# The MLP products of a two-layer decoder trunk by Strassen's scheme, up and down as two phases

## The chip, the cores and the metric

The kernel runs on one core of a Trainium2 chip. The metric is the time of one execution on the device in microseconds (us). The engines are named as the profile names them: PE multiplies matrices (PEld is its weight load), DVE, ACT and POOL work element by element, SP only issues DMAs here.

## What is computed

Two layers over 1024 positions of width 1024; the change touches the MLP at the end of each.

```python
for l in range(DEPTH):                      # DEPTH = 2, D_MODEL = 1024, D_FF = 4096
    h = rms_norm(x, norm1[l])
    proj = h @ w_in[l]                      # pool | gate u, v | q, k, v
    ...                                     # pooling, spatial gate, stick-breaking attention
    x = x + jnp.concatenate([ya, yb, yc], axis=-1) @ w_out[l]
    h = rms_norm(x, norm2[l])
    x = x + jnp.square(jax.nn.relu(h @ w_up[l])) @ w_down[l]
return rms_norm(x, final_norm)
```

All data are float32. Each product is computed from operands split in two float32r parts, a high and a low one, as three products: high by high, high by low, low by high.

## The kernel before

Everything is held transposed: a tile has 128 channels on the partitions and 512 positions (half `c`, 1 or 0) in its free dimension, so x is 8 x 2 tiles (`k`, `c`). `mm3` issues the three matmuls of 128 x 128 weights by a 128 x 512 tile into one PSUM bank for each contraction tile. Weights come as 512 KB tiles `raw` through SP (two buffers); `split` makes the high part on ACT (`copy`) and the low part on DVE (`tensor_sub`). The order on each engine is set by the Tile scheduler from the program order and priorities (`early`); it is fixed when the kernel is built, and each engine runs its list in order.

`out_proj(0, second)` is the last step before the MLP: for each of 16 (m, c), twelve matmuls into a bank `po`, then DVE adds the residual (L731), ACT and DVE make the scaled high and low parts that the MLP will read (`put_x`, L115 and L117), ACT squares and POOL adds the square to the running sum `rbc` (L136), from which `rms` later makes the norm of every position.

The MLP runs 8 groups of 4 hidden tiles of 128. For each hidden tile `f` and half `c` there are 24 matmuls into a bank `pj` (`proj`), DVE evacuates with relu and the norm (L776), ACT squares (L780), POOL squares as well (L781), DVE subtracts (L783). Then, for each output tile (m, c), twelve matmuls over the group's four hidden tiles into a bank `po`, and DVE adds the bank to the residual tile `xa` (L800). In one layer that is 1536 matmuls up and 1536 down. The banks rotate: `pj` 2, `po` 4, `pg` 2. In the very last group the positions are split in three pieces (`TAIL`), so that the final norm of one overlaps the products of the next.

## Time and profile before

| | |
|---|---|
| median of 3 runs | 2351.18 us (2351.13 to 2353.78) |
| profiled execution, its own time | 2353.58 us |
| its span in the trace | 2351.9 us |
| TensorE's mean granted clock | 0.984 |
| PE busy | 2268.2 us, 96% of the span |
| DVE, ACT, POOL busy | 54%, 31%, 35% |
| moved by DMA | 118.41 MB |

A profile's groups give, for a line, an engine and an operation, the number of instructions, the mean time of one, and what ended the idle time ahead of them. A busy PE counts a matmul from its start to the end of its pipeline, so the time between two starts, not the duration, is what one more matmul costs. The windows give the busy time of each engine in a stretch.

### The profile page before, as it was taken

How to read it: one execution, taken by the hardware profiler on the slowest of the kernel's cores; microseconds unless marked ns; L12 is line 12 of the kernel's file. 1: busy time of each engine (PE TensorE's matmuls, PEld its weight loads, DVE VectorE, ACT ScalarE, POOL GpSimd, SP SyncE). 2: the span in 40 equal slices, each digit the busy share in tenths (PEclk: the TensorE clock that was granted, in tenths of full speed). 3: DMA queues.
4: the chain of work that ended last, by engine and by line, in shares of the span. 5: the costliest groups of instructions: out<-in, count | busy, mean ns of one | idle time of the engine just before them, and what ended most of it. 6: DMA issues, size and time to landing. Idle time of an engine off the chain costs nothing.

```text
span 2351.9 us, 28573 instructions
## 1 busy us (share of the span) xinstructions
PE 2268.2 (96%) x11224; PEld 1917.9 (82%) x11224; DVE 1264.1 (54%) x1606; ACT 725.5 (31%) x1321; POOL 824.4 (35%) x889
## 2 busy tenths in 40 slices
PE   7999989999999999999999898999999999999997
PEld 5988887788888888888888887878888888888887
DVE  8787769842342342342558777796433433332334
ACT  5556553430120120121446555434110110120121
POOL 7667656430110110111347767464110110110115
PEclk9999999999999999999999998999999999999998
DMA  3000103120220120120301010131210210220211
GB/s 126 28 28 28 42 19 95 54 81 9 63 72 15 58 72 18 54 72 19 125 19 45 11 45 24 41 90 45 72 47 28 69 55 27 63 63 19 63 36 72
DMA packets 40247, 118.41 MB, mean 50 GB/s; under 512 B 5040, under 2 KB 7600, under 8 KB 40112
## 3 DMA queue, kind: packets, MB, share of 16 engines
q1 hardware_dynamic: 38448, 114.48, 15.9%
q8 instruction: 88, 1.44, 0.3%
q10 hardware_dynamic: 1664, 2.10, 0.2%
q14 instruction: 47, 0.39, 0.1%
HBM read 108.17 MB, written 8.39 MB: 50 GB/s over the span
## 4 chain that ended last, share of the span: by engine, by line
PE 79%; DVE 9%; POOL 6%; issue 3%; ACT 2%; DMA 0%; SPq 0%; POOLq 0%; DVEq 0%; ACTq 0%
PE pj L191 13%; PE pj L196 13%; PE pj L197 13%; PE po L197 12%; PE po L196 12%; PE po L191 11%; DVE s L372 3%; POOL a L375 2%; PE t L393 2%; PE av L403 1%; PE av L404 1%; POOL s L365 1%; POOL a L365 1%; PE z L356 1%; PE z L357 1%
## 5 line engine op out<-in xcount | busy, mean ns | idle before, releaser
L781 POOL TENSOR_TENSOR tmp<-tmp 128x512 f32<-128x512 f32 x128 | 177.4, 1386 | 1125.3 <-ACT ah L780 1118.1
L196 PE MATMUL pj<-xl,wh 128*128 128x512 f32 x1344 | 525.4, 391 | 2.8 <-DVE xl L117 2.8
L191 PE MATMUL pj<-xh,wh 128*128 128x512 f32 x1344 | 526.1, 391 | 0.0
L197 PE MATMUL pj<-xh,wl 128*128 128x512 f32 x1344 | 524.9, 391 | 0.0
L191 PE MATMUL po<-ah,dh 128*128 128x512 f32 (+1 forms) x1056 | 402.0, 383 | 1.2 <-DVE xa L800 1.2
L197 PE MATMUL po<-ah,dl 128*128 128x512 f32 (+1 forms) x1056 | 401.9, 383 | 0.0
L196 PE MATMUL po<-al,dh 128*128 128x512 f32 (+1 forms) x1056 | 401.9, 383 | 0.0
L800 DVE TENSOR_TENSOR xa<-po,xa 128x512 f32<-128x512 f32 (+1 forms) x264 | 177.8, 675 | 412.2 <-PE po L197 412.0
L780 ACT ACTIVATE ah<-tmp 128x512 fp32r<-128x512 f32 x128 | 80.3, 628 | 728.3 <-DVE tmp L776 728.3
L196 PEld LDWEIGHTS pj<-xl,wh 128*128 128x128 f32 x1344 | 253.0, 188 | 54.9 <-DVE xl L117 3.7
L197 PEld LDWEIGHTS pj<-xh,wl 128*128 128x128 f32 x1344 | 252.7, 188 | 51.4
L191 PEld LDWEIGHTS pj<-xh,wh 128*128 128x128 f32 x1344 | 253.0, 188 | 51.0
L375 POOL TENSOR_TENSOR a<-a,s 128x255 f32<-128x255 f32 (+1 forms) x192 | 221.3, 1155 | 28.7 <-DVE s L372 21.2
L191 PEld LDWEIGHTS po<-ah,dh 128*128 128x128 f32 x1056 | 198.5, 188 | 40.1 <-DVE xa L800 1.4
L196 PEld LDWEIGHTS po<-al,dh 128*128 128x128 f32 x1056 | 198.6, 188 | 38.6
L197 PEld LDWEIGHTS po<-ah,dl 128*128 128x128 f32 x1056 | 198.6, 188 | 38.6
L776 DVE SCALAR_TENSOR_TENSOR tmp<-pj,rbc 128x512 f32<-128x512 f32 x124 | 85.5, 689 | 207.7 <-PE pj L197 197.9
L108 ACT CAST wh<-raw 128x1024 fp32r<-128x1024 f32 x116 | 121.8, 1050 | 204.4 <-PE pj L196 146.9
L109 DVE TENSOR_TENSOR wl<-raw,wh 128x1024 fp32r<-128x1024 f32 x116 | 154.2, 1329 | 33.1 <-ACT wh L108 32.3
L783 DVE TENSOR_TENSOR al<-tmp,ah 128x512 fp32r<-128x512 f32 x128 | 90.1, 705 | 146.0 <-POOL tmp L781 146.0
L372 DVE TENSOR_TENSOR_SCAN s<-s 128x256 f32<-128x256 f32 (+3 forms) x128 | 132.3, 1041 | 54.4 <-POOL s L365 52.9
L108 ACT CAST dh<-raw 128x1024 fp32r<-128x1024 f32 x64 | 67.2, 1049 | 206.7 <-DMA raw<-in_w_down 206.7
(169 smaller groups left out, 3547.5 us busy)
## 6 DMA issues: line engine op xcount, KB each, us to landing
raw<-in_w_up SPq DMA_DIRECT2D x64, 512.0 KB, 3.6
raw<-in_w_down SPq DMA_DIRECT2D x64, 512.0 KB, 3.6
raw<-in_w_in SPq DMA_DIRECT2D x36, 512.0 KB, 3.6
raw<-in_w_out SPq DMA_DIRECT2D x16, 512.0 KB, 3.6
tmp<-in_xT SPq DMA_DIRECT2D x16, 256.0 KB, 2.7
xd<-xa SPq DMA_DIRECT2D x16, 256.0 KB, 2.0
tmp<-xd SPq DMA_DIRECT2D x16, 256.0 KB, 2.7
a<-in_xT SPq DMA_DIRECT2D x12, 256.0 KB, 5.3
```

What stands on the lines that cost most here:

```text
L108: nc.scalar.copy(hi, src)
L109: nc.vector.tensor_sub(lo, src, hi.bitcast(F32))
L191: mm = nc.tensor.matmul(ps, ah, bh, start=first and i == 0, stop=False)
L196: nc.tensor.matmul(ps, ah, bl, start=False, stop=False)
L197: nc.tensor.matmul(ps, al, bh, start=False, stop=last and i == n - 1)
L372: nc.vector.tensor_tensor_scan(sl, sl, sl, 1.0 if prev is None else prev[:, CH - 1 : CH], ALU.mult, ALU.bypass)
L375: nc.gpsimd.tensor_mul(a[:, lo + 1 : CH], a[:, lo + 1 : CH], s[:, lo : CH - 1])
L776: nc.vector.scalar_tensor_tensor(out=r, in0=ps, scalar=0.0, in1=rbc[c], op0=ALU.max, op1=ALU.mult)
L780: nc.scalar.activation(h, r, AF.Square)
L781: nc.gpsimd.tensor_mul(r, r, r)
L783: nc.vector.tensor_sub(lo, r, h.bitcast(F32))
L800: nc.vector.tensor_add(x, ps, x)
```

## The change

**Products.** A 2 x 2 block product of weights A (A11, A12, A21, A22) and data B takes seven block products, where it took eight: the seven of the Winograd form of Strassen's scheme. They are listed in `STEPS`, each with its accumulating bank (X, Y, Z), the weight block and the data block:

```diff
+STEPS = (
+    ("X", 0, "A11", "B11"), ("Y", 0, "A12", "B21"), ("X", 1, "S2", "T2"), ("Z", 0, "S1", "T1"),
+    ("X", 2, "S3", "T3"), ("Z", 1, "S4", "B22"), ("X", 3, "A22", "T4"),
+)
```

X takes four of them in a row and is read out after each, before the next is added to it (`skip_group_check`). S1 to S4 are sums of weight blocks, made on POOL (`load_a`); T1 to T4 are sums of data blocks.

**Up phase.** An *up step* takes two hidden tiles (A: 2 hidden by 2 channel tiles; B: 2 channel tiles by 2 halves): 7 x 12 = 84 matmuls where two hidden tiles took 96. There are 16 in a layer. The four output blocks of hidden activations, and T1 to T4 for the next phase, are written to DRAM (`hid`), seven tiles of 256 KB a step.

**Down phase.** A *down step* takes four hidden tiles by half of the output tiles, again 84 matmuls for 96; there are 16 in a layer, two to a group. It reads seven tiles of 256 KB back and splits them (`load_b`). Products are added to accumulators in SBUF (`add_to`); the results in Y and Z go through an ACT copy and are added on POOL (`lent`). In the second layer the last group is left as it was (`classic`), because of its `TAIL`.

**Ahead of the MLP.** `second` writes the residual to DRAM and makes seven blocks for each pair of channel tiles (B11, B21, B22 and T1 to T4) where `put_x` made four. The low parts of T1 to T4 are made on POOL (L839).

```diff
+            def load_a(srcs, n):
+                for src in srcs:
+                    raws.append(per.tile([P, D], F32, tag="raw", name=nm("raw"), bufs=2))
+                    nc.sync.dma_start(raws[-1].rearrange("p (f c) -> p f c", f=src.shape[1]), src)
...
+                with early(W_EARLY):
+                    split(*room("w", ("A11", "A12"), per, 2, turns), top)
+                    s12 = ex.tile([P, D], F32, tag="s", name=nm("s12"), bufs=1)
...
+                    nc.gpsimd.tensor_add(s1, a2[:, 0], a2[:, 1])
+                    nc.gpsimd.tensor_sub(s2, s1, a1[:, 0])
+                    split(*room("w", ("S1", "S2"), per, 2), s12)
+                    s3 = tmp()
+                    nc.gpsimd.tensor_sub(s3.rearrange("p (n w) -> p n w", n=n), a1[:, 0], a2[:, 0])
+                    split(*room("u", ("S3",), mw, 1), s3)
+                    nc.gpsimd.tensor_sub(a2[:, 0], s2, a1[:, 1])
+                    split(*room("v", ("S4", "A22"), mw, 1, turns), low)
...
+            def second(m, c, ps):
+                x = t512("xa", 6, F32, xs_)
+                nc.vector.tensor_add(x, ps, x1[m, c])
+                nc.sync.dma_start(xmid[m, c], x)
+                add_sq(m, c, x)
...
+                    t = t512("xt", 3, F32, xs_)
+                    nc.vector.scalar_tensor_tensor(out=t, in0=src, scalar=g, in1=in1, op0=ALU.mult, op1=op)
+                    nc.scalar.copy(h, t)
+                    nc.gpsimd.tensor_sub(lo, t, h.bitcast(F32))
...
+                    def hidden(b, src, c):
+                        r, h = ct(), ct()
+                        nc.vector.scalar_tensor_tensor(
+                            out=r, in0=src, scalar=0.0, in1=rbc[c], op0=ALU.max, op1=ALU.mult
+                        )
+                        nc.gpsimd.tensor_mul(h, r, r)
...
+                            if (bank, i) == ("X", 0):
+                                kept["P1"] = keep(ps)
+                            elif bank == "Y":
+                                t = ct()
+                                nc.vector.tensor_add(t, ps, kept["P1"])
+                                hidden("B11", t, 1)
+                            elif (bank, i) == ("X", 1):
+                                kept["U2"] = keep(ps)
...
+                                    mixed("T1", "B11", "B12", nc.vector.tensor_sub)
+                                    mixed("T2", "B22", "T1", nc.vector.tensor_add)
+                                    mixed("T3", "B22", "B12", nc.vector.tensor_sub)
...
+                def load_b(fp, names):
+                    for b in names:
+                        raw = t512("hr", 4, F32, md)
+                        nc.sync.dma_start(raw, hid[fp, b])
+                        h, lo = out[b] = block_tiles(b)
+                        with early(EVAC_EARLY):
+                            split(h, lo, raw)
+                def add_to(m, c, ps, sign, lent):
+                    x = acc_[m, c]
+                    eng, src = nc.vector, ps
+                    if lent:
+                        eng, src = nc.gpsimd, tmp()
+                        nc.scalar.copy(src, ps)
+                    (eng.tensor_add if sign > 0 else eng.tensor_sub)(x, x, src)
```

**Where it moves instructions.** In all, PE has 8688 of the matmuls that `mm3` issues where it had 9432. Three places show the new order. On PE, in the up phase of the first layer, before: the end of one hidden tile's 24 matmuls (bank `pj_6448`) and the start of the next (`pj_6480`, another bank):

```order
L191 MATMUL pj_6448<-xh_5111,wh_6373 128x512
L196 MATMUL pj_6448<-xl_5113,wh_6373 128x512
L197 MATMUL pj_6448<-xh_5111,wl_6374 128x512
L191 MATMUL pj_6480<-xh_4808,wh_6373 128x512 [waits DVE_49]
L196 MATMUL pj_6480<-xl_4810,wh_6373 128x512
L197 MATMUL pj_6480<-xh_4808,wl_6374 128x512
```

After, at a like place in the up phase: the end of X's second product (S2 in `wh_6134`, T2 in `eh`) and the start of its third (S3 in `uh_6140`, T3):

```order
L210 MATMUL po_6231<-eh_5369,wh_6134 128x512
L215 MATMUL po_6231<-el_5370,wh_6134 128x512
L216 MATMUL po_6231<-eh_5369,wl_6135 128x512
L210 MATMUL po_6231<-eh_5021,uh_6140 128x512 [waits Activation_49]
L215 MATMUL po_6231<-el_5022,uh_6140 128x512
L216 MATMUL po_6231<-eh_5021,ul_6141 128x512
```

The two products now stand back to back on the same bank, with a wait for ACT's copy of the first between them; 30 of the 32 up steps have this pair so.

On DVE, in the down phase of the first layer, before (`xa` is the residual tile, `al`, `wl` and `dl` are low parts):

```order
L109 TENSOR_TENSOR dl_7588<-raw_7586,dh_7587 128x1024
L783 TENSOR_TENSOR al_7534<-tmp_7529,ah_7531 128x512
L776 SCALAR_TENSOR_TENSOR tmp_7561<-pj_7536,rbc_5174 128x512
L109 TENSOR_TENSOR wl_7818<-raw_7816,wh_7817 128x1024
L783 TENSOR_TENSOR al_7566<-tmp_7561,ah_7563 128x512
L800 TENSOR_TENSOR xa_4785<-po_7592,xa_4785 128x512
L800 TENSOR_TENSOR xa_4827<-po_7620,xa_4827 128x512
```

After (L127 are low parts of weights, `wl`, `ul`, `vl`, and of tiles read back, `hr`; L993 are additions to an accumulator):

```order
L993 TENSOR_TENSOR acc_8061<-acc_8061,po_9355 128x512
L127 TENSOR_TENSOR wl_9419<-s_2044_9415,wh_9418 128x1024
L993 TENSOR_TENSOR acc_8065<-acc_8065,po_9358 128x512
L127 TENSOR_TENSOR el_9688<-hr_9685,eh_9687 128x512
L127 TENSOR_TENSOR ul_9425<-tmp_9422,uh_9424 128x512
L127 TENSOR_TENSOR el_9848<-hr_9845,eh_9847 128x512
L127 TENSOR_TENSOR xl_9854<-hr_9851,xh_9853 128x512
L993 TENSOR_TENSOR acc_8035<-acc_8035,po_9539 128x512
L993 TENSOR_TENSOR acc_8059<-acc_8059,po_9355 128x512
L993 TENSOR_TENSOR acc_8039<-acc_8039,po_9542 128x512
L127 TENSOR_TENSOR xl_9866<-hr_9863,xh_9865 128x512
```

The additions that free the banks stand between splits, where they had stood alone in long rows; a down step has 8 of them, 8 splits of 512 and 3 of 1024.

On POOL, in `out_proj(0, second)`, before (the two running sums in turn):

```order
L136 TENSOR_TENSOR rbc_4791<-rbc_4791,tmp_4833 128x512
L136 TENSOR_TENSOR rbc_4812<-rbc_4812,tmp_4855 128x512
L136 TENSOR_TENSOR rbc_4791<-rbc_4791,tmp_4883 128x512
L136 TENSOR_TENSOR rbc_4812<-rbc_4812,tmp_4905 128x512
L136 TENSOR_TENSOR rbc_4791<-rbc_4791,tmp_4927 128x512
```

After (L154 is the running sum, L839 a low part of T1 to T4, L794 a sum of weight blocks):

```order
L839 TENSOR_TENSOR xl_5084<-xt_5085,xh_5083 128x512
L154 TENSOR_TENSOR rbc_4959<-rbc_4959,tmp_5128 128x512
L839 TENSOR_TENSOR el_5136<-xt_5137,eh_5135 128x512
L839 TENSOR_TENSOR el_5142<-xt_5143,eh_5141 128x512
L794 TENSOR_TENSOR s_1115_5400<-raw_5394 128x512
L154 TENSOR_TENSOR rbc_4937<-rbc_4937,tmp_5175 128x512
L839 TENSOR_TENSOR el_5148<-xt_5149,eh_5147 128x512
```

POOL's list there grows from 14 additions to 34 instructions (14 sums, 16 low parts, 4 sums of weight blocks), and the sums that the norm needs stand behind low parts.

## Rows read from the trace of the kernel before

**Rows 1.** Page: span; busy us (share of the span), instructions of an engine.

```profile
span 2351.9 us, 28573 instructions
...
PE 2268.2 (96%) x11224; PEld 1917.9 (82%) x11224; DVE 1264.1 (54%) x1606; ACT 725.5 (31%) x1321; POOL 824.4 (35%) x889
```

**Rows 2.** Windows: stretch in us, busy us and instructions of each engine, clock, DMA.

```profile
core 0: us, PE busy (x) PEld busy (x) DVE busy (x) ACT busy (x) POOL busy (x), PEclk, DMA share, GB/s
438.00:480.00 42.00, 42.00 (x186) 34.20 (x185) 32.79 (x38) 23.31 (x36) 20.11 (x15) 1.00 0.18 51
800.00:1000.00 200.00, 200.00 (x884) 165.65 (x883) 70.05 (x90) 25.51 (x32) 22.34 (x16) 1.00 0.14 43
1190.00:1215.00 25.00, 22.46 (x140) 19.71 (x141) 16.02 (x25) 14.25 (x30) 12.96 (x22) 0.93 0.15 43
...
500.00:1190.00 690.00, 690.00 (x3049) 571.64 (x3047) 258.08 (x328) 117.58 (x155) 105.65 (x79) 1.00 0.18 55
```

**Rows 3.** Timeline, DVE, down products: start us, duration us, instruction, [idle before <-releaser].

```profile
536.73 0.69 DVE L800 TENSOR_TENSOR xa<-po,xa 128x512 f32<-128x512 f32 x1 [2.03 <-PE po L197]
539.45 0.69 DVE L800 TENSOR_TENSOR xa<-po,xa 128x512 f32<-128x512 f32 x1 [2.03 <-PE po L197]
```

**Rows 4.** Groups by line and shape: xcount | busy us, mean ns | idle before.

```profile
L191 PE MATMUL po<-ah,dh 128*128 128x512 f32 x992 | 383.7, 389 | 0.0
...
L800 DVE TENSOR_TENSOR xa<-po,xa 128x512 f32<-128x512 f32 x248 | 171.3, 691 | 402.7 <-PE po L197 402.6
...
L783 DVE TENSOR_TENSOR al<-tmp,ah 128x512 fp32r<-128x512 f32 x128 | 90.1, 705 | 146.0 <-POOL tmp L781 146.0
...
L109 DVE TENSOR_TENSOR dl<-raw,dh 128x1024 fp32r<-128x1024 f32 x64 | 78.4, 1226 | 62.1 <-ACT dh L108 62.1
```

**Rows 5.** Timeline, second layer's `rms`: a PSUM bank handed from PE to ACT.

```profile
1641.05 1.05 PE L163 MATMUL pg<-ident,rst 128*128 128x128 f32 x8
...
1642.19 0.59 ACT L165 COPY rbc<-pg 128x512 f32<-128x512 f32 x1 [9.52 <-PE pg L163]
```

**Rows 6.** Timeline, second layer's attention: a PSUM bank handed back from ACT to PE.

```profile
1206.71 0.38 ACT L362 ACTIVATE a<-z 128x256 f32<-128x256 f32 x1
...
1207.14 0.33 PE L356 MATMUL z<-kx,qh 128*128 128x128 f32 x1 [0.40 <-ACT a L362]
```

**Rows 7.** Timeline, DVE in `out_proj(0, second)` of the first layer.

```profile
443.23 0.74 DVE L117 SCALAR_TENSOR_TENSOR xl<-xa,cs,xh 128x512 fp32r<-128x512 f32 x1
443.89 0.68 DVE L731 TENSOR_TENSOR xa<-po,xh 128x512 f32<-128x512 f32 x1
444.49 4.58 DVE L117 SCALAR_TENSOR_TENSOR xl<-xa,cs,xh 128x512 fp32r<-128x512 f32 x3
...
451.13 0.69 DVE L731 TENSOR_TENSOR xa<-po,xh 128x512 f32<-128x512 f32 x1
```

**Rows 8.** Timeline, POOL in the same stretch.

```profile
443.47 5.05 POOL L136 TENSOR_TENSOR rbc<-rbc,tmp 128x512 f32<-128x512 f32 x3 [6.74 <-ACT tmp L132]
451.10 1.30 POOL L136 TENSOR_TENSOR rbc<-rbc,tmp 128x512 f32<-128x512 f32 x1 [2.57 <-ACT tmp L132]
```

**Rows 9.** Timeline, first layer's `rms`: the power on POOL.

```profile
479.46 1.02 POOL L153 TENSOR_TENSOR rst<-rst,mhalf 128x4 f32<-128x4 f32 x1 [1.89 <-DVE rst L149]
```

**Rows 10.** DMA issues: queue, xcount, KB each, median us from issue to landing.

```profile
raw<-in_w_up SPq DMA_DIRECT2D x64, 512.0 KB, 3.6
...
xd<-xa SPq DMA_DIRECT2D x16, 256.0 KB, 2.0
tmp<-xd SPq DMA_DIRECT2D x16, 256.0 KB, 2.7
```

More of the change, by code (lines that the diff above doesn't have):

```diff
@@ L185, in trunk_kernel, with mm3 @@
         pace = []
-        def mm3(ps, wx, first, last):
+        def mm3(ps, wx, first, last, more=False):
             n = len(wx)
             for i, ((ah, al), (bh, bl)) in enumerate(wx):
-                mm = nc.tensor.matmul(ps, ah, bh, start=first and i == 0, stop=False)
+                mm = nc.tensor.matmul(ps, ah, bh, start=first and i == 0, stop=False, skip_group_check=more)
                 if pace and first and i == 0:
@@ L195, in mm3 @@
                     )
-                nc.tensor.matmul(ps, ah, bl, start=False, stop=False)
-                nc.tensor.matmul(ps, al, bh, start=False, stop=last and i == n - 1)
+                nc.tensor.matmul(ps, ah, bl, start=False, stop=False, skip_group_check=more)
+                nc.tensor.matmul(ps, al, bh, start=False, stop=last and i == n - 1, skip_group_check=more)
         def proj(w, c, bank=None):
@@ L239, in trunk_kernel @@
                 xres[1, k, c] = xd.tile([P, CH], F32, tag=f"xd{k}{c}", name=f"xd_{k}_{c}")
+        xmid = {(k, c): xd.tile([P, CH], F32, tag=f"xm{k}{c}", name=f"xm_{k}_{c}") for k in range(KT) for c in (1, 0)}
+        hid = {
+            (fp, b): xd.tile([P, CH], F32, tag=f"hd{fp}{b}", name=f"hd_{fp}_{b}")
+            for fp in range(NFP) for b in BLOCKS + ("B12",)
+        }
         order = []
@@ L244, in trunk_kernel @@
             order += [w_out[l, i] for i in (4, 5, 6, 7, 0, 1, 2, 3)]
-            order += [w_up[l, i] for i in range(NFT)]
+            order += [None]
         ready = []
         def prefetch():
-            if order:
+            if order and order[0] is not None:
                 ready.append(load_w(order.pop(0)))
@@ L553, in trunk_kernel @@
             misc[0] = psg
-            yq = tc.tile_pool(name=f"yq{l}", bufs=1, side="right", reuse_waits="tile")
+            yq = tc.tile_pool(name=f"yq{l}", bufs=1, reuse_waits="tile")
             yq_ = yq.__enter__()
@@ new lines, in load_a, with room @@
+            def load_a(srcs, n):
+                raws = []
+                for src in srcs:
+                    raws.append(per.tile([P, D], F32, tag="raw", name=nm("raw"), bufs=2))
+                    nc.sync.dma_start(raws[-1].rearrange("p (f c) -> p f c", f=src.shape[1]), src)
+                top, low = raws
+                turns = "p (n k w) -> p k n w"
+                a1, a2 = (r.rearrange(turns, n=n, k=2) for r in raws)
+                out = {}
+                def room(tag, names, pool, bufs, by=None):
+                    two = [
+                        pool.tile([P, CH * len(names)], F32R, tag=tag + x, name=nm(tag + x), bufs=bufs) for x in "hl"
+                    ]
+                    for i, b in enumerate(names):
+                        out[b] = tuple(
+                            t.rearrange(by or "p (k n w) -> p k n w", n=n, k=len(names))[:, i] for t in two
+                        )
+                    return two
+                with early(W_EARLY):
+                    split(*room("w", ("A11", "A12"), per, 2, turns), top)
+                    s12 = ex.tile([P, D], F32, tag="s", name=nm("s12"), bufs=1)
+                    s1, s2 = (s12[:, i * CH : (i + 1) * CH].rearrange("p (n w) -> p n w", n=n) for i in range(2))
+                    nc.gpsimd.tensor_add(s1, a2[:, 0], a2[:, 1])
[6 more added lines that the diff above has]
+                    split(*room("v", ("S4", "A22"), mw, 1, turns), low)
+                return out
@@ new lines, in trunk_kernel, with products @@
+            out_proj(0, second)
+            xsp.__exit__(None, None, None)
+            yq.__exit__(None, None, None)
+            misc[0] = psg
+            def products(a, b, banks, step, q):
+                bank, i, an, bn = STEPS[step]
+                ah, al = a[an]
+                mm3(
+                    banks[bank],
+                    [(tuple(t[:, p, q * P : (q + 1) * P] for t in (ah, al)), x[bn]) for p, x in enumerate(b)],
+                    i == 0, True, i > 0,
+                )
+                return bank, i
```

232 lines of the change are left out of this document (180 added, 52 removed).

## The prediction, made before the run

> **What bounds the kernel now.** I read the page's head first: PE is busy 2268.2 of 2351.9 us, DVE 54%, ACT 31%, POOL 35% [rows 1]. Then the windows, to see whether that holds in the MLP: from 800 to 1000 us PE is busy all 200.0 us for 884 matmuls, and no other engine passes 70.05 us [rows 2]. So the MLP is PE alone, and a matmul there costs 200/884 = 0.226 us. The additions to `xa` say the same: each follows twelve matmuls and they start 539.45 − 536.73 = 2.72 us apart, 0.2265 a matmul, and before each DVE has waited 2.03 us for PE [rows 3]. Weights never bound it: DMA has a share of 0.14 to 0.18 [rows 2]. `out_proj(0, second)` of the first layer (438 to 480 us) is PE-bound as well, but DVE is at 32.79 of 42.00 us there, its highest [rows 2].
>
> What is gained is thus counted on PE, and what may be lost is whatever makes PE idle for the first time. The sum is made on the profiled execution (2353.6 us), which lies 2.4 us above the median of the runs; I take 2.4 off at the end.
>
> **A. Matmuls removed.** PE's list has 9432 − 8688 = 744 fewer matmuls of 128 x 512: 744 x 0.2265 = **−168.5 us**. A step of 84 then takes 84 x 0.2265 = 19.03 us.
>
> **B. X handed over in the up phase.** In 30 up steps X's second and third product stand back to back, and the third waits for ACT's copy of the second. Before has no such wait in the MLP. I build it: the last matmul runs to its end, 0.39 us [rows 4]; ACT starts 1642.19 − (1641.05 + 1.05) = 0.09 after a bank's last matmul and copies for 0.59 [rows 5]; PE starts 1207.14 − (1206.71 + 0.38) = 0.05 after ACT has let go of a bank [rows 6]. Sum 1.12, less the 0.2265 that the next matmul would have taken anyhow: 0.89 x 30 = **+26.8**. Its bounds are 0.6 and 2 us (ACT busy with another copy), +18 to +60. Other bank changes have a product of another bank between them, at least 12 x 0.2265 = 2.7 us.
>
> **C. The rest of the up phase.** DVE has per step three weight splits of 1.23 [rows 4] and twelve operations of 512 at about 0.69 [rows 4]: 12.0 us of 19.9. POOL's eight come to 8 x 1.30 = 10.4 [rows 8]. The long one is the weight chain: S3, S4 and A22 have one buffer, free only when X's last product ends; then come a split, the load (3.6 us [rows 10]), three POOL sums, the next split. I get a slack near 2 us of 19. I take 0.2 x 30 = **+6** (0 to 30).
>
> **D. The down phase.** Per step DVE has three weight splits of 1.23, eight splits of 512 at 0.70 and eight additions at 0.69 [rows 4], 14.8 us; POOL has ten operations of 1.30 [rows 8], 13.0 us. Both fit in 19.03 if they don't disturb each other. They do: in `out_proj` three `xl` took 4.58 us on DVE beside three POOL additions of 5.05 [rows 7, 8]. Alone they are 3 x 0.74 and 3 x 1.30, so DVE lost (4.58 − 2.22)/3 = 0.79 for each and POOL (5.05 − 3.90)/3 = 0.38. The addition from a bank at 451.13 is not slowed beside POOL's at 451.10: 0.69 and 1.30 [rows 7, 8]. So an operation with both inputs in SBUF pays, one from PSUM doesn't. [...]
>
> How often they meet: 11 of a down step's 19 DVE operations, 58%, have both inputs in SBUF. A POOL operation then costs DVE 0.58 x 0.79 = 0.46, ten of them 4.6: 14.8 + 4.6 = 19.4 us, where PE has 19.03. I hold this against the stretch of 438 to 480: 16 additions, 16 `xl` and 4 weight splits are 16 x 0.69 + 16 x 0.74 + 4 x 1.23 = 27.8 us alone, and DVE was busy 32.79 beside 15 POOL instructions [rows 2], +0.33 each with DVE idle 22% of the time. A DVE that is full has no idle time to hide in, so 0.46 is fair. At 19.4 of 19.03 with waits between the lists, I take 20.0 us a step: +1.0 on the 26 of 30 down steps that read tiles back, **+26**. Bounds: 0 (all fits) and 14.8 + 10 x 0.79 = 22.7, +95.
>
> **E. From `out_proj` into the MLP.** There DVE goes to 16 additions, 28 `xl`-like operations and 4 weight splits: 11.0 + 20.7 + 4.9 = 36.7 us; POOL from 14 sums to 34 instructions [rows 2, 8]. By the same rule 32 of 48 DVE operations can pay: 34 x 0.79 x 0.67 = 18.0, together 54.7. PE has 16 x 12 x 0.2265 = 43.5. The first up product needs the last of these blocks, and the norm needs POOL's last sum, then the matmul 0.39, copy 0.59 and power 1.02 [rows 5, 9], some 2 us. 54.7 + 2 − 43.5 = 13 a layer, **+26** (10 to 40).
>
> **F. From up to down.** The products now wait for a way through DRAM: T4 is made last, its write stands on SP ahead of the reads; a write takes 2.0 and a read 2.7 us [rows 10], then ACT's and DVE's split, about 6 us to the first product. Only four `hr` buffers exist, so the eighth to tenth reads come 12 to 15 us later. Other products and the accumulators' loads can fill part of it; I take 8.5 us of idle PE. [...] About 10 a layer, **+20** (12 to 32).
>
> **G. Layer's end and tail.** The last additions go through ACT and POOL (0.59 + 1.30) before the next layer's norm, and `classic` must take over: **+8** (0 to 16).
>
> Sum: 2353.6 − 168.5 + 26.8 + 6 + 26 + 26 + 20 + 8 = 2297.9, less 2.4: **2296 us**. DMA about doubles, with 14 more tiles of 256 KB for an up and a down step, but before it has a share of 0.18 at most in these views; I price it at nothing, and if it did not hide, reads would show as waits of F's kind in every step.
>
> **The rivals.** *1. The contention hides.* Scheduling lets POOL run where DVE adds from banks; C and D are 0 and E is 5 a layer: 2351.2 − 168.5 + 26.8 + 10 + 20 + 8 = 2247. For it: before, with DVE 78% busy, PE lost nothing from 438 to 480 [rows 2], and banks in the down phase have some 20 matmuls, over 4 us, until they are needed again. Against it: 19.4 of 19.03 leaves no room to catch up.
>
> *2. Slower: DVE and POOL take turns.* Each operation of DVE with both inputs in SBUF excludes POOL's. Then a down step needs 3 x 1.23 + 8 x 0.69 = 9.2 on DVE and 13.0 on POOL in turn, 22.2 us: +3.2 x 26 = 83; `out_proj` 20.7 + 4.9 + 34 x 1.30 = 69.8, +2 − 43.5 = 28 a layer, 57; up steps nearly full as well, 10 in place of 6. 2351.2 − 168.5 + 26.8 + 10 + 83 + 57 + 20 + 8 = 2388. It decides from where a down step costs 21.5 us with E at 40: 2351.2 − 168.5 + 27 + 6 + 26 x 2.5 + 40 + 20 + 8 = 2349. For it: in the burst of [rows 7, 8] both engines slowed, not DVE alone. Against it: full turns would make each pair 0.74 + 1.30 = 2.04 us, where the burst shows 4.58/3 = 1.53 on DVE and 5.05/3 = 1.68 on POOL, so they overlap in part. [...]
>
> *3. The weight chain binds* (C's slack is negative): +2 us on 56 steps over the forecast's C and D, 2296 + 112 − 33 = 2375.
>
> That the change would not do what it says is out: the 744 matmuls are gone from PE's list.
>
> **How the numbers follow.** Forecast 0.50, its own range 2262 to 2335 (D from 0 to +60, with C, E and F a few us to either side). Rival 1: 0.22, rival 2: 0.17, rival 3: 0.06, others 0.05. About 0.2% (2346.5 to 2355.9) is what a measurement of this kernel can tell from no change. Faster holds the forecast and rival 1, nearly all of it, and a little of the others: 0.73. Slower holds rivals 2 and 3 less their lower ends: 0.22. Same: 0.05. The range that leaves about 2 in 10 out goes from somewhat under rival 1 to just under rival 2: 2240 to 2385.
>
> **What the profile after would show.** A: 0.2265 us between matmuls inside a product, everywhere in the MLP. B: some 0.9 us of idle PE once per up step, ended by the copy on ACT. C: no PE wait for weight splits in the up phase; under rival 3 there is one a step, ended by a split of S3, S4 or A22. D: in a window over down steps DVE busy above 0.95, POOL's mean for 512 columns over 1.5 us, steps near 20 us, and PE waits ended by DVE; under rival 1 DVE stays below 0.9 with no such wait, under rival 2 steps pass 21.5. E: DVE busy throughout `out_proj`, and PE idle for 10 us or more before the first up products, ended by DVE or POOL. F: one gap of 6 us or more per layer, ended by the split of an `hr` tile, with a granted clock below 1.00. I would be wrong at the root if matmuls that read two products into one bank ran at another pace, or if DMA waits stood in every step.

## The result, and the profile after

| | before | after |
|---|---|---|
| median | 2352.5 us (4 runs) | 2412.0 us (4 runs, 2410.3 to 2413.6) |
| span of the profiled execution | 2351.9 us | 2409.6 us |
| PE busy | 2268.2 us, 96% | 2178.9 us, 90% |
| DVE, ACT, POOL busy | 54%, 31%, 35% | 72%, 43%, 63% |
| moved by DMA | 118 MB | 250 MB |

The changed kernel takes 1.0252 times as long (95% interval 1.0234 to 1.0270). The forecast was 2296 us, faster than before, the range 2240 to 2385. The 744 matmuls are gone and with them 168.5 us of PE's work; so some 226 us of new loss came with them, where the sum had 113.

The head of the page after, which answers [rows 1]:

```profile
span 2409.6 us, 30641 instructions
...
PE 2178.9 (90%) x10480; PEld 1783.8 (74%) x10480; DVE 1743.9 (72%) x2064; ACT 1032.6 (43%) x1847; POOL 1527.5 (63%) x1349
```

Windows of after by stage, as in [rows 2]: the end of `out_proj` and the first up step, the up steps between, the way from up to down, and the down steps, of the first layer; then the same four of the second. (Columns: stretch, busy us and instructions of PE, PEld, DVE, ACT, POOL, the granted clock, DMA's share, GB/s.)

```profile
429.50:523.00 93.50, 82.48 (x342) 65.32 (x341) 77.50 (x78) 41.87 (x66) 69.16 (x44) 0.93 0.25 88
523.00:804.80 281.80, 269.15 (x1142) 212.12 (x1142) 154.29 (x200) 70.29 (x95) 140.88 (x108) 1.00 0.42 140
804.80:924.80 120.00, 89.34 (x341) 67.29 (x340) 81.65 (x99) 50.15 (x80) 56.98 (x39) 0.89 0.60 199
924.80:1193.90 269.10, 246.49 (x1042) 193.36 (x1041) 217.50 (x227) 126.99 (x205) 203.09 (x129) 1.00 0.40 121
1617.30:1710.90 93.60, 82.55 (x343) 65.44 (x342) 77.49 (x79) 42.22 (x67) 69.13 (x44) 0.93 0.27 89
1710.90:1992.00 281.10, 269.09 (x1142) 212.17 (x1141) 154.08 (x199) 70.02 (x94) 139.93 (x108) 1.00 0.43 140
1992.00:2105.00 113.00, 86.77 (x338) 66.33 (x337) 80.06 (x90) 49.40 (x78) 57.37 (x39) 0.89 0.59 196
2105.00:2330.00 225.00, 206.19 (x871) 161.65 (x870) 183.47 (x190) 104.39 (x170) 169.47 (x106) 1.00 0.40 121
```

Such a table gives the loss of a stage at once: its length less its matmuls by 0.2265 us. The up steps: 281.8 − 1142 x 0.2265 = 23.1 us in 13.6 steps, 1.7 a step. The down steps: 269.1 − 236.0 = 33.1 us in 12.4 steps, 2.7 a step, and 225.0 − 197.3 = 27.7 in 10.4 steps in the second layer, again 2.7. The way from up to down: 120.0 − 339 x 0.2265 = 43 us and 113.0 − 336 x 0.2265 = 37 us (short matmuls left out), of which one ordinary up step and three down steps would lose some 10. The first window holds 34 short matmuls besides 308 long ones: 93.5 − 308 x 0.2265 = 23.7 us, where before lost about 5 at the same place (in the second layer 23.6).

What PE waited for, after (engine, bank and line, releaser's line, us in total, times, longest):

```profile
PE po L210 <- DVE acc L993: 39.0, 30, 5.7
PE po L210 <- ACT xh L126: 30.0, 4, 12.3
PE po L216 <- DVE wl L127: 24.3, 17, 3.2
PE po L210 <- ACT ct L893: 23.4, 32, 1.8
```

Before, the down products had waited 1.2 us in all. Now there is a line for each stage: most of `acc` and of `wl` (low parts of weights) is the down phase, `xh` (tiles read back) the way from up to down, and `ct` the hand-over of X.

### The profile page after: what moved, and what is told of

It reads as the page before. It is cut to its first block, busy times and chain, and to the rows that moved or that the text cites. A ratio compares the mean times of both kernels' runs of the same rounds, so it can differ in the third digit from the quotient of the medians.

```text
span 2409.6 us, 30641 instructions
## 1 busy us (share of the span) xinstructions
PE 2178.9 (90%) x10480; PEld 1783.8 (74%) x10480; DVE 1743.9 (72%) x2064; ACT 1032.6 (43%) x1847; POOL 1527.5 (63%) x1349
## 5 line engine op out<-in xcount | busy, mean ns | idle before, releaser
L902 POOL TENSOR_TENSOR ct<-ct 128x512 f32<-128x512 f32 x128 | 167.4, 1309 | 303.8 <-issue 165.8
L993 POOL TENSOR_TENSOR acc<-acc,tmp 128x512 f32<-128x512 f32 x180 | 300.0, 1682 | 89.0 <-ACT tmp L992 88.2
L127 DVE TENSOR_TENSOR wl<-s,wh 128x1024 fp32r<-128x1024 f32 x62 | 93.2, 1504 | 229.5 <-ACT wh L126 229.5
L215 PE MATMUL pj<-xl,wh 128*128 128x512 f32 x600 | 237.1, 395 | 2.8 <-DVE xl L135 2.8
L210 PE MATMUL pj<-xh,wh 128*128 128x512 f32 x600 | 236.4, 396 | 0.2 <-ACT xh L126 0.2
L216 PE MATMUL pj<-xh,wl 128*128 128x512 f32 x600 | 233.2, 393 | 0.0
L127 DVE TENSOR_TENSOR wl<-raw,wh 128x1024 fp32r<-128x1024 f32 x114 | 173.2, 1520 | 40.2 <-ACT wh L126 39.1
L993 DVE TENSOR_TENSOR acc<-acc,po 128x512 f32<-128x512 f32 x240 | 158.9, 676 | 54.9 <-POOL acc L993 45.4
L794 POOL TENSOR_TENSOR s<-raw 128x512 f32<-128x512 f32 x62 | 82.2, 1327 | 157.2 <-DMA raw<-in_w_down 106.8
L127 DVE TENSOR_TENSOR xl<-hr,xh 128x512 fp32r<-128x512 f32 x128 | 140.1, 1104 | 40.4 <-ACT xh L126 40.4
L215 PEld LDWEIGHTS pj<-xl,wh 128*128 128x128 f32 x600 | 113.9, 190 | 28.2 <-DVE xl L135 3.7
L210 PEld LDWEIGHTS pj<-xh,wh 128*128 128x128 f32 x600 | 114.2, 190 | 24.2 <-ACT xh L126 1.0
L216 PEld LDWEIGHTS pj<-xh,wl 128*128 128x128 f32 x600 | 113.5, 189 | 23.2
```

The costliest lines, as they stand in the source:

```text
L127: nc.vector.tensor_sub(lo, src, hi.bitcast(F32))
L210: mm = nc.tensor.matmul(ps, ah, bh, start=first and i == 0, stop=False, skip_group_check=more)
L215: nc.tensor.matmul(ps, ah, bl, start=False, stop=False, skip_group_check=more)
L216: nc.tensor.matmul(ps, al, bh, start=False, stop=last and i == n - 1, skip_group_check=more)
L794: nc.gpsimd.tensor_add(s1, a2[:, 0], a2[:, 1])
L902: nc.gpsimd.tensor_mul(h, r, r)
```

## The experiments

Each is the changed kernel with the edit shown, but for one that edits the kernel before. `early` and the `NOSYNC` dependencies are there for the order of an engine's list alone. A `...` in a diff stands for lines left out.

### The down phase: chain or contention

The down phase was forecast by DVE's load, 19.4 us a step. The trace shows DVE waiting for POOL as well: X's third product is added by DVE to the accumulator to which POOL adds Z's first. DVE's timeline, after (start us, duration us, instruction, [idle before <-releaser]):

```profile
1054.69 1.78 DVE L127 TENSOR_TENSOR xl<-hr,xh 128x512 fp32r<-128x512 f32 x1 [0.19 <-ACT xh L126]
1058.92 0.69 DVE L993 TENSOR_TENSOR acc<-acc,po 128x512 f32<-128x512 f32 x1 [2.45 <-POOL acc L993]
```

POOL's at the same time:

```profile
1055.88 1.75 POOL L798 TENSOR_TENSOR tmp<-raw,raw 128x512 f32<-128x512 f32 x1
1057.60 1.29 POOL L993 TENSOR_TENSOR acc<-acc,tmp 128x512 f32<-128x512 f32 x1
```

DVE stands still for 2.45 us while POOL first makes a sum of weights and then the addition. Two runs take this apart.

**down_scratch**: POOL's work stays, nobody waits for it.

```diff
-                        eng, src = nc.gpsimd, tmp()
+                        src = tmp()
                         nc.scalar.copy(src, ps)
+                        nc.gpsimd.tensor_add(scratch, src, src)
+                        return
```

> The changed kernel, with the additions that POOL makes in the down phase (six to a step) changed so that POOL adds the same two-input work into a scratch tile that nobody reads; the terms of Y and Z are thus left out of the result. POOL's load and its reads of SBUF stay, but DVE no longer waits for POOL's addition to the same accumulator. Theory chain (DVE's wait of 24.5 us for POOL's additions in 12.4 steps is what makes a down step take about 2.7 us over 84 matmuls): some 2 us a step come back, 26 to 30 steps, 50 to 60 us, near 2357. Theory contention (DVE's splits are slow beside POOL's reads): DVE's busy time in a step stays near 17.5 us, PE still waits for it, and the time falls by less than 20 us.

Measured: 2377.5 us, 34.5 less than the changed kernel: between the two expectations.

**down_nopool**: the same without the line on POOL.

> The changed kernel without POOL's additions of Y's and Z's terms in the down phase (ACT's copies stay); these terms are left out of the result. Six of POOL's ten operations in a step go. Theory contention: DVE's operations with two SBUF inputs come down from 1.2 towards 0.8 us for 512 columns, DVE's busy time in a step from 17.5 to 16 us or less, and the time falls by 50 us or more, clearly below the run with the scratch tile. Theory chain: the time is that of the run with the scratch tile, within 8 us.

Measured: 2337.0 us, 75 less than the changed kernel and 40 less than with the scratch tile. So neither theory alone: the chain is worth some 35 us, POOL's additions as load another 40 once the chain is gone. (The split is not exact: an addition into the scratch tile reads one tile twice and took POOL 1.40 us, where one into an accumulator took 1.65.)

**pool_memset**: the line is `nc.gpsimd.memset(scratch, 0.0)`, twice.

> As down_scratch, but where POOL adds two tiles it clears the scratch tile twice: POOL is about as long at work and writes SBUF, but reads none. Y's and Z's terms are left out of the result here too. Theory (POOL's reads of SBUF are what slows DVE's operations with two SBUF inputs): time and DVE's durations are those of down_nopool, 2330 to 2342. Rival (any work of POOL on SBUF slows DVE, or the ACT copies wait for POOL): near down_scratch, 2370 or above.

Measured: 2337.5 us, as without POOL's additions. A stretch of the down phase as a window, after:

```profile
940.00:1120.00 180.00, 162.07 (x682) 126.39 (x682) 148.59 (x155) 84.86 (x139) 129.54 (x82) 1.00 0.44 132
```

The same stretch in down_scratch:

```profile
940.00:1120.00 180.00, 169.06 (x714) 132.46 (x713) 153.71 (x165) 90.56 (x148) 120.97 (x87) 1.00 0.45 136
```

In down_nopool:

```profile
940.00:1120.00 180.00, 180.00 (x781) 146.56 (x780) 133.32 (x175) 97.25 (x153) 51.08 (x36) 1.00 0.45 140
```

And in pool_memset:

```profile
940.00:1120.00 180.00, 180.00 (x781) 146.47 (x780) 134.11 (x178) 98.41 (x156) 91.14 (x114) 1.00 0.47 141
```

A group of DVE's splits there by line and shape (xcount | busy us, mean ns of one | idle before), after:

```profile
L127 DVE TENSOR_TENSOR el<-hr,eh 128x512 fp32r<-128x512 f32 x26 | 29.4, 1144 | 0.0
```

In down_scratch:

```profile
L127 DVE TENSOR_TENSOR el<-hr,eh 128x512 fp32r<-128x512 f32 x28 | 31.9, 1151 | 0.0
```

In down_nopool:

```profile
L127 DVE TENSOR_TENSOR el<-hr,eh 128x512 fp32r<-128x512 f32 x26 | 20.8, 812 | 0.0
```

And in pool_memset, where POOL clears tiles:

```profile
L127 DVE TENSOR_TENSOR el<-hr,eh 128x512 fp32r<-128x512 f32 x28 | 22.1, 801 | 0.0
```

PE's matmuls divided by 84 are the steps in the 180 us: 8.1, 8.5, 9.3 and 9.3, so a step takes 22.2, 21.2, 19.4 and 19.4 us. DVE's busy time a step is 18.3, 18.1, 14.3 and 14.4. Six additions of POOL thus cost DVE 18.1 − 14.3 = 3.8 us, 0.63 each; clearing tiles, POOL works 40 us more in this stretch than without its additions, and DVE's step stays at 14.4 us against 14.3. What the additions have and the clearing lacks is, by the code, reads of SBUF: a split `el` took 1151 ns beside the additions, 801 beside the clearing and 812 with neither.

In these steps DVE was not full in the changed kernel, 148.59 of 180 us. It is late, not short of time: its list is served in order, and a split that takes 1.14 us for 0.7, or a wait for POOL, delays what stands behind it. That is the addition which frees the bank PE wants next, or the low part of the next weights. PE's waits in the same 180 us, after (us in total, times, longest):

```profile
PE po L210 <- DVE acc L993: 9.9, 10, 1.7
PE po L216 <- DVE wl L127: 8.3, 7, 1.7
```

In down_scratch they are 8.0 and 2.8 us: by these waits, what the chain had cost there is for the most part late weights. In down_nopool PE is busy all 180.00 us.

**down_z0**: one argument; DVE adds Z's first product, out of the bank.

```diff
-                                        add_to(m0 + 2, 0, ps, -1, True)
+                                        add_to(m0 + 2, 0, ps, -1, False)
```

> The changed kernel with one thing changed: in the down phase the term of Z's first product is added by DVE out of the bank, not by ACT and POOL. It is the addition whose accumulator DVE needs next (X's third product). DVE then has ten additions of 0.69 a step, POOL eight operations. Theory (the chain between POOL and DVE cost 34 us in the run with the scratch tile, and this link is most of it): 20 to 35 us less, near 2385. Rival (DVE is full, two more additions a step cost what the chain gives back): within 10 us of 2412.

Measured: 2368.6 us, 43 less, and less time than either expectation. DVE no longer waits for POOL's addition in the down phase at all. It gave more than the scratch run's 35; that fits two of POOL's additions a step being gone as well (a split `el` takes 1037 ns for 1144), but the two were not tried apart. The same stretch in down_z0:

```profile
940.00:1120.00 180.00, 175.97 (x748) 140.75 (x748) 163.52 (x191) 84.12 (x135) 112.87 (x72) 0.99 0.47 144
```

DVE is busier than in the changed kernel, 91% for 83%, and PE idles less.

**down_dve**: all additions on DVE (`if lent:` becomes `if False:`).

> The changed kernel with all fourteen additions of a down step on DVE, out of the banks: POOL has four operations a step and ACT no copies of banks. DVE has 3 x 1.23 + 8 x 0.70 + 14 x 0.69 = 18.9 us a step. Theory (what POOL's reads cost DVE is worth about what an addition costs DVE itself): little difference to down_z0, 2360 to 2380. Rival (DVE is the bound once it has all the additions): 18.9 + 4 x 0.46 = 20.8 us a step, 1 us more than in down_z0, 2390 or above.

Measured: 2340.1 us, 72 less: faster than the kernel before (0.9938, 0.9918 to 0.9958), by this edit alone. Both expectations were too high. The same stretch in down_dve:

```profile
940.00:1120.00 180.00, 178.98 (x775) 145.47 (x775) 163.61 (x231) 67.76 (x96) 51.81 (x37) 1.00 0.44 141
```

Two groups of DVE there, additions from banks at 0.67 us and splits at 0.72:

```profile
L993 DVE TENSOR_TENSOR acc<-acc,po 128x512 f32<-128x512 f32 x76 | 49.2, 674 | 1.9 <-PE po L216 1.9
L127 DVE TENSOR_TENSOR el<-hr,eh 128x512 fp32r<-128x512 f32 x26 | 18.4, 719 | 0.0
```

775/84 = 9.2 steps: DVE is busy 17.7 us of a step of 19.5, with six additions more than in the changed kernel and 0.6 us less of work. An addition lent to POOL had cost DVE 0.63 us, about what it costs when DVE makes it itself, and the wait on top.

### The hand-over of X in the up phase

PE after, the end of X's second product and the start of its third:

```profile
613.08 0.40 PE L216 MATMUL po<-eh,wl 128*128 128x512 f32 x1
614.15 0.50 PE L210 MATMUL po<-eh,uh 128*128 128x512 f32 x1 [0.68 <-ACT ct L893]
```

1.07 us from start to start, 0.84 more than a matmul, and the same in all 30 steps: the forecast was 0.89.

**up_strict**: from the second step on, the first matmul of a product is put behind the last of the product ahead of it in `STEPS`.

```diff
+                if strict and i == 0 and chain:
+                    tc.add_manual_dep(
+                        mm.ins, chain.pop(), mybir.DependencyInfo(NOSYNC, mybir.DependencyReason.DATA), reason="order"
+                    )
...
+            if strict:
+                chain.append(mm.ins.name)
```

> The changed kernel with one thing changed: from the second up step of a layer on, the products stand on PE in the order in which STEPS lists them, so that Z's product stands between X's second and third. Theory (the hand-over of X is a wait of its own): the gap of 1.07 us between the last matmul of X's second product and the first of the third becomes 0.23, and the kernel takes 30 x 0.85 = 25 us less, near 2387. Rival (what the gap hides, the weights and the evacuations, ends late next): the gap goes, other waits of about the same size come up, and the time stays within 8 us of 2412.

Measured: 2410.9 us, 1 less. The gap is gone there and stands, longer, ahead of X's second product. PE of up_strict:

```profile
587.14 0.39 PE L222 MATMUL pj<-xh,wl 128*128 128x512 f32 x1
588.92 0.50 PE L212 MATMUL po<-eh,wh 128*128 128x512 f32 x1 [1.40 <-ACT ct L901]
```

And its ACT:

```profile
587.34 1.04 ACT L126 CAST wh<-raw 128x1024 fp32r<-128x1024 f32 x1 [4.38 <-PE pj L221]
588.29 0.58 ACT L901 COPY ct<-po 128x512 f32<-128x512 f32 x1
```

The bank was complete a product earlier, at about 584.8, but its copy stands on ACT behind a split that waits for the weight buffer which Y's product still reads. ACT's wait of 4.38 us ahead of the split held up the copy behind it.

**up_strict2**: `with early(2000):` around the copy.

> As up_strict, and ACT's copies of banks in the up phase (P1, U2, P5) go ahead of the next weights' splits in ACT's list. In up_strict the gap had moved: X's second product waited 1.39 us for the copy of the first, which stood on ACT behind a split that waits for a weight buffer to come free. Theory: with the copy first, both gaps are gone, a step takes 84 x 0.230 = 19.4 us where it took 20.35, and the kernel takes 25 us less, near 2386. Rival (the splits, now later, end late): PE waits for a weight split instead, and the time stays within 8 us of 2411.

Measured: 2410.6 us. No list changed, ACT's least of all: the program's instructions are those of up_strict in the same order. So this run says nothing on the theory.

**up_strict3**: as up_strict, and the split is put behind the copy in ACT's list.

```diff
+                    cast = nc.scalar.copy(h, top)
+                    if after:
+                        tc.add_manual_dep(
+                            cast.ins, after, mybir.DependencyInfo(NOSYNC, mybir.DependencyReason.DATA), reason="order"
+                        )
```

> As up_strict, and the split of the next A11 and A12 on ACT is held, in ACT's list, behind the copy of X's first product (in up_strict2 the list on ACT had stayed as it was). Theory (the hand-over of X is PE's only wait in a step, and it moves to whatever stands ahead of the copy on ACT): now no gap of X is left, a step takes 84 x 0.230 = 19.4 us and not 20.35 to 21.0, and the kernel takes 25 to 30 us less than the changed kernel, near 2385. Rival (the weights' chain is next, within 1 us): a wait for a split of weights of 0.5 to 1 us a step takes its place, and the time stays within 10 us of 2411.

Measured: 2364.0 us, 48 less. ACT of up_strict3 now copies ahead of the split:

```profile
565.71 0.59 ACT L907 COPY ct<-po 128x512 f32<-128x512 f32 x1 [1.92 <-PE po L222]
568.21 1.06 ACT L800 CAST wh<-raw 128x1024 fp32r<-128x1024 f32 x1 [1.91 <-PE pj L221]
```

PE has no gap in the steps from 560 to 604 us, 19.3 us each; in the changed kernel a step took 20.3 to 21.3, in up_strict 21.0. From X's third product in a layer's first up step to that in its last, the two layers are 13.5 and 15.0 us shorter, 28 in sum: that is what the theory forecast. The other 20 were not expected and have other places. From X's third product in the last up step to that in the first down step it takes 7 and 4 us less (43.5 for 50.9, and 42.2 for 46.2); up_strict has this too (43.8 and 42.5), so it goes with PE's order and not with ACT's. Some 7 more lie between the first layer's down phase and the second layer's up phase; what they are was not tried.

### From up to down

SP ahead of the first down product, after:

```profile
840.25 0.32 SPq L905 DMA_DIRECT2D hd_B<-ct  x1
840.98 0.32 SPq L911 DMA_DIRECT2D hd_T<-ct  x1
841.39 0.90 SPq L980 DMA_DIRECT2D hr<-hd_B  x2
```

PE's first down product:

```profile
846.77 1.22 PE L210 MATMUL po<-xh,wh 128*128 128x512 f32 x2 [11.67 <-ACT xh L126]
```

The reads start 0.4 us after T4's write and the first product 5.8 us after it, as the prediction had it. PE is busy 22.83 of 42.0 us there, and the granted clock is 0.81, with 1.00 up to 827 us and 0.50 from 838.1 us on:

```profile
804.80:846.80 42.00, 22.83 (x86) 16.82 (x84) 20.54 (x28) 8.64 (x11) 19.69 (x17) 0.81 0.46 156
```

**f_early**: the four buffers `hr` lie in a pool of their own that is free in the up phase, and the first four reads are issued in the last up step's place in the program.

```diff
+            hrp = tc.tile_pool(name=f"hr{l}", bufs=1, reuse_waits="tile")
...
+                        if step == 0 and fp == NFP - 1:
+                            for b in BLOCKS[:4]:
+                                fetch(0, b)
```

> The changed kernel with one thing changed: the four buffers for tiles read back lie in space that the up phase doesn't use, so that the first reads of the down phase are issued during the last up steps and the splits follow as their buffers come free; before, the space came free with the last write of the up phase, and the reads stood on SP behind that write. Theory (late reads make the idle of 19 to 23 us of PE between the last up product and the second down step): 15 to 25 us a layer come back, near 2370. Rival (the loads are bound by DMA there, 300 to 400 GB/s from 846 to 875 us, or the accumulators, now behind the reads, come late): 0 to 10 us in all.

Measured: 2404.9 us, 7 less. Down products now begin inside the last up step, and then PE stops. PE of f_early:

```profile
870.47 0.79 PE L210 MATMUL po<-eh,wh 128*128 128x512 f32 x1 [15.97 <-DVE acc L1004]
```

SP of f_early:

```profile
862.90 0.92 SPq L884 DMA_DIRECT2D hr<-hd_T  x2
863.87 8.95 SPq L1012 DMA_DIRECT2D acc<-xm  x14
```

The accumulators' loads had come to stand behind the reads of the second group. So the gain is the rival's size, and by one of the rival's reasons.

**f_order**: as f_early, and a dependency puts the second group's reads behind these loads; of the loads the first half is issued ahead of the products and the second half during the first group's products.

```diff
+                if fp in (2, 3):
+                    tc.add_manual_dep(
+                        dma.ins, last_acc[-1], mybir.DependencyInfo(NOSYNC, mybir.DependencyReason.DATA), reason="order"
+                    )
...
+                load_acc(0)
...
+                            if step == 1 and u == 0 and g == 0:
+                                load_acc(4)
```

> As f_early, but the second group's reads stand on SP behind the loads of the accumulators. In f_early the first down products began during the last up step, and PE then waited 16 us for the first accumulator, whose load stood behind 28 reads. Theory (the order on SP alone makes that wait): the 16 us come back in both layers, 2405 - 30 = 2375. Rival (DMA's rate is the limit, 8 MB at 300 to 400 GB/s are 20 to 27 us in either order): within 10 us of 2405.

Measured: 2390.8 us, 14 less than f_early, 21 less than the changed kernel. Between the two expectations: the wait is 8.4 us where it was 16. PE of f_order:

```profile
861.71 0.80 PE L210 MATMUL po<-eh,wh 128*128 128x512 f32 x1 [8.38 <-DVE acc L1008]
```

The order of the loads, and their being halved, took away half of the wait; how much of the rest is DMA's rate was not tried.

### Ahead of the up phase

**e_memset**: POOL clears the low parts of T1 to T4 there in place of computing them.

```diff
-                    nc.gpsimd.tensor_sub(lo, t, h.bitcast(F32))
+                    nc.gpsimd.memset(lo.bitcast(F32), 0.0)
```

> The changed kernel, with the low parts of the mixed data blocks T1 to T4 ahead of the MLP cleared by POOL and not computed (the MLP's up products lose their low parts by that; the number of products stays). 16 of POOL's 34 instructions there no longer read SBUF and take about 0.6 us in place of 1.3. Theory (DVE is the bound from 430 to 481 us, at 48 of 51 us, and 16 x 0.48 = 8 us of that is POOL's doing): about 6 to 8 us a layer come back, 2397 to 2402. Rival (DVE's own 36.7 us and the order of the lists set the end): less than 6 us in all.

Measured: 2390.9 us, 21 less, 10.5 a layer: more than half of what the stage lost over before. POOL's part is real and larger than priced. DVE of e_memset is as busy from 430 to 481 us as it was, with 57 instructions done where 49 were; it is nearly full, as the prediction said. After:

```profile
429.50:480.90 51.40, 44.52 (x190) 34.91 (x188) 48.16 (x49) 24.55 (x41) 38.99 (x23) 0.99 0.26 93
```

And e_memset:

```profile
429.50:480.90 51.40, 50.23 (x221) 40.37 (x221) 47.33 (x57) 29.62 (x48) 31.29 (x32) 1.00 0.30 103
```

### The pace of a matmul

After, in a product of A12 and B21 (bank `pj`) and in the next, of S2 and T2:

```profile
608.47 0.39 PE L210 MATMUL pj<-xh,wh 128*128 128x512 f32 x1
...
610.29 0.39 PE L216 MATMUL pj<-xh,wl 128*128 128x512 f32 x1
610.51 0.39 PE L210 MATMUL po<-eh,wh 128*128 128x512 f32 x1
...
613.08 0.40 PE L216 MATMUL po<-eh,wl 128*128 128x512 f32 x1
```

Eight matmuls in 1.82 us are 0.2275 each, eleven in 2.57 are 0.2336. I put the time from one matmul's start to the next one's against the places that the program gives the tiles in SBUF (KB are 1000 bytes of a partition). In the kernel before, products of x with `wh` and `wl`, the data 3 to 80 KB above the weights, take 0.2272 us; `out_proj`, 116 to 161 KB above, 0.2333. In the changed kernel T2 to T4 on `wh`, over 130 KB above, take 0.2332. But distance is not the whole rule, and the expectation below, "under some 50 KB" and "above 110 KB", is too simple: products on `vh` with the data 21 to 87 KB below take 0.2324, those on `uh` with the data 57 to 103 above 0.2316; and x on `wh`, in the same places as before, takes 0.2284. The mean in the changed kernel's MLP is 0.2307, in that of the kernel before 0.2267.

**before_far**: the kernel before, with the tiles `wh` and `wl` at the other end of SBUF (213 to 229 KB).

```diff
+        far = ctx.enter_context(tc.tile_pool(name="far", bufs=1, side="right"))
...
-            pool = pool or per
+            pool = pool or far
```

> The kernel before with one thing changed: the tiles of weights that most products use (16 KB a partition) lie at the other end of SBUF, far from the tiles x (high and low) that they multiply, 110 KB or more, where they lay beside them. Nothing else moves. Theory distance (the pace of a matmul depends on how far its weights and its data lie apart in SBUF: 0.2268 us under some 50 KB, 0.2333 above 110 KB in both traces): the 4032 matmuls on x take 4 to 6 ns longer each, the 768 of the projection after the attention up to 6 ns less, in sum 11 to 20 us more than before, 2363 to 2372. Rival (the pace has another cause, the load on the other engines or the kind of tile): the time stays within 4 us of before.

Measured: 2358.3 us against 2353.9, 1.0019 (1.0008 to 1.0031): the direction is right, the size a third of it, and by the time alone the rival (within 4 us) is hardly out. The pace itself tells more. (One more thing moved: with 16 KB of weights gone to the other end, every other tile lies 16 KB lower, at the same distances from one another.) Windows of before, in `out_proj` and in the MLP:

```profile
430.00:470.00 40.00, 40.00 (x173) 32.26 (x173) 32.05 (x41) 19.30 (x30) 15.60 (x11) 1.00 0.19 53
500.00:1170.00 670.00, 670.00 (x2957) 554.95 (x2956) 255.05 (x324) 115.09 (x151) 99.79 (x72) 1.00 0.18 55
```

And of before_far:

```profile
430.00:470.00 40.00, 40.00 (x178) 32.93 (x177) 31.27 (x39) 20.54 (x32) 16.90 (x12) 1.00 0.18 53
500.00:1170.00 670.00, 670.00 (x2943) 552.16 (x2942) 253.28 (x322) 114.71 (x150) 98.23 (x71) 1.00 0.18 55
```

PE is never idle in either, so the counts are the pace: faster in `out_proj`, whose data now lie near the weights, slower in the MLP. Matmul by matmul, those on `xh` with the high weights stay at 0.2272 us, with the low weights they go from 0.2272 to 0.2310, those on `xl` from 0.2271 to 0.2294; `out_proj` falls from 0.2333 to 0.2278. With 1344 of each on x and 256 of each in `out_proj` that is 8 − 4 = +4 us, what was measured. So the place changed the pace here, the rest being the same; which property of the place, and what in the chip does it, stays open.

### The edits together

**combo** (up_strict2, down_z0, f_early, and the accumulators loaded where first needed):

> The changed kernel with the edits of up_strict2, down_z0 and f_early together, and the loads of the accumulators placed where each is needed first. If the three losses add up (25, 28 and 35 us): 2412 - 88 = 2324, faster than the kernel before by 1.2%. If they cover each other or move on: 2360 to 2400, no faster than before.

Measured: 2352.7 us, 0.9992 (0.9982 to 1.0002): neither. up_strict2 alone had given nothing of the 25 us counted for it.

**combo2** (up_strict3, down_z0, f_order):

> The edits of up_strict3, down_z0 and f_order together on the changed kernel. If up_strict3 and f_order work as their theories say, 2369 - 27 - 37 = 2305, faster than the kernel before by 2%; if only one of them does, 2330 to 2345; if neither, 2350 to 2360.

Measured: 2316.8 us, 0.9839 (0.9823 to 0.9856): between the first case and the second.

**combo3** (up_strict3, down_dve, f_order):

> As combo2, with all additions of the down phase on DVE as in down_dve. If the edits add up: 2412 - 48 - 72 - 21 = 2271; if down_dve's gain over down_z0 (29 us) adds to combo2: 2317 - 29 = 2288; if DVE, now with the splits of the tiles read back and all additions, becomes the bound: 2305 or above.

Measured: 2300.4 us, 0.9768 (0.9752 to 0.9785): 2.3% faster than the kernel before, and 112 us less than the changed kernel. The three gains sum to 141; 29 are lost between them, and the time lies between the second case and the third. In the down phase PE is full (combo3):

```profile
940.00:1150.00 210.00, 209.34 (x903) 169.11 (x903) 183.48 (x254) 80.22 (x114) 66.66 (x47) 1.00 0.42 132
```

and so it is in the up steps (219.83 of 220 us from 560 to 780). What is left lies at the ends of the phases and in the pace, not in the steps.

## The prediction, point by point

Losses over both layers, by the windows above (the pace of 0.2307 in place of 0.2265 is in each stage; it is some 22 us in all):

| step | forecast | measured |
|---|---|---|
| A, matmuls | −168.5 | −168.5 |
| B, hand-over of X, 30 times | +26.8 | 30 x 0.84 = +25 |
| C, rest of the up phase | +6 | 30 x (1.7 − 0.84) = +26, about 10 of it pace |
| D, down phase | +26 | 30 x 2.7 = +80, about 10 of it pace |
| E, ahead of the up phase | +26 | 2 x 19 = +38 |
| F, from up to down | +20 | 33 + 27 = +60 |
| G, the remainder of the 57.7 us between the spans | +8 | −3 |

**What bounds the kernel, and A**, were right as far as they went: the matmuls are gone. The step that failed in A is "a matmul there costs 0.2265", taken over to operands in other places of SBUF, where it cost 0.2307 on average. The trace of before held the warning: `out_proj` runs at 0.2333 a matmul.

**B** was right in its size, the wait built from four rows of other places. It was not right as a removable item of its own: up_strict moved it, and only with ACT's list changed as well did the up steps give back 28 us.

**C** was too small by 20 us. Some 10 of its 26 are pace, and some 10 are PE's waits for the low part of S1 (bank `pg`, 0.5 us in 9 of 13 steps of the first layer): the sign "no PE wait for weight splits in the up phase" failed.

**D is the step with the largest miss,** 54 of the 113 us that were lost beyond the sum; F has 40, C 20, E 12. With D alone put right the forecast would have been some 2350, no faster than before. D added up DVE's load (19.4 us forecast; 18.3 measured) and took a step as that plus 0.6 for "waits between the lists", 20.0; a step took 21.7. That 19.4 came near is in part luck: an addition of POOL cost DVE 0.63 us and not 0.46, while the load alone was too high, since it sums durations that overlap by some 0.08 us (443.23 + 0.74 against 443.89 in [rows 7]). What failed is the step from load to time: an engine need not be full to be late. DVE was busy 83% of these steps, where the sign set for D was above 95%; the other two signs, POOL's mean over 1.5 us (1.65) and PE waits ended by DVE, came. Two things made DVE late: the chain over the accumulator from POOL to DVE, which the code and the order show and for which the sum has at most those 0.6 us (some 35 us in all), and the slowed operations in DVE's list ahead of the additions that free banks and of the low parts of weights (some 40 us). Rival 1 rested on some 4 us until a bank is needed again; the waits used these up.

**Rival 2** (slower, by turns of DVE and POOL) had the right sign and nearly the right price for a down step, 22.2 us. Its mechanism is a part of the cause only: DVE and POOL overlapped (18.3 and 16.0 us of work in a step of 22.2), and taking the chain away gave back 35 us with POOL's six additions a step still there. That the price fits is luck as far as the chain goes.

**E** had the right mechanism. It was too small by 12 us, and not by one long wait: the gap before the first up products is 5.1 us, where the sign said 10 or more. POOL's low parts alone are 21 us (e_memset). And the clock fell, which the forecast had not priced there: after that gap, from 481.5 to 486.2 us, the granted clock is 0.50 and the matmuls start 0.43 us apart, where they start 0.23 apart ahead of it, and over the first window the granted clock is 0.93.

**F** named the right things, a write ahead of the reads and the buffers, and was too small by 40 us. The guess that "other products and the accumulators' loads can fill part of it" failed: the loads of the accumulators hold the products up (f_early, f_order), and the granted clock was 0.89 over 120 and 113 us. Of the 10 us a layer that the forecast took, 8.5 are idle PE; the other 1.5, for a lower clock, are the author's estimate, a term that no run shows by itself. What after shows is a granted clock of 0.50 from 846.8 to 851.6 us, where most matmuls start 0.43 us apart, and of 1.00 from 909.8 to 924.8, where 66 of them start in 15.0 us. How much of the 40 is the clock, how much the order and how much DMA's rate stays open; f_order gave back 21. **Rival 3** did not come: no wait for S3, S4 or A22 stands in the up steps. (Its sum takes off 33 for C and D, which are 32.)

## What to carry to other kernels

When a scheme takes work from the engine that was always busy, ask of each bank or buffer which list frees it, what stands ahead of that instruction there, and whom that waits for in turn; loads that fit in the time say little (DVE was busy 83% of the down steps here, and late). An addition lent to a second engine is a gain only if nobody needs its result soon and it doesn't slow the lender: here it cost the lender 0.63 us, and doing it takes 0.67. A wait that is removed by reordering one engine can reappear where another engine's list has the old order, as X's did here (1.40 us in up_strict), and then both have to move.

## What was new of the hardware

The time of a 128 x 512 matmul hung on where its operands lie in SBUF: moving the tiles `wh` and `wl` alone to the other end took `out_proj` from 0.2333 to 0.2278 us a matmul and products on x from 0.2272 to as much as 0.2310 (before_far). Distance alone does not set it: products of the changed kernel with weights and data within 87 KB of one another had anything from 0.2284 to 0.2324. 41 us of POOL clearing tiles in 180 left DVE's splits `el` at 801 ns (pool_memset), where they took 812 without (down_nopool); 74 us of its additions took them to 1151 ns (down_scratch).
